# A fourth group of seven products in the feed-forward of a two-layer encoder kernel

## The chip, the cores and the metric

The kernel runs as one program on one core of one Trainium2 chip. The metric is the device time of an execution in microseconds (us), lower is better. All products are computed from float32 weights and activations, and the result must be the reference's.

## The reference

The kernel computes two layers of an encoder over 256 tokens of width 1024. Each layer has a gated linear attention, an ordinary attention, a merge of the two, a feed-forward part (FFN) and a per-layer embedding. What matters here is the FFN:

```
D_MODEL, SEQ, DEPTH = 1024, 256, 2
FFN_HIDDEN = 2816
...
gate, up = jnp.split(rms_norm(h, g_ffn_pre) @ w_ffn_in, 2, axis=-1)
h = h + rms_norm((jax.nn.silu(gate) * up) @ w_ffn_out, g_ffn_post)
```

`w_ffn_in` is 1024 x 5632 and `w_ffn_out` 2816 x 1024, for each layer. The merge before it ends in the products with `w_o_attn`, `w_o_gla` and `w_out`, each 1024 x 1024.

## The kernel before, in words

**Products.** TensorE multiplies a float32 product as three products of fp32r numbers: every operand is split into a high part and a rest, and high x high, high x low and low x high are added in one bank of PSUM (`mm3`, L99; the instruction is at L97). The program calls a product's weights `wh` and `wl`, and its accumulator `acc`.

**The stream of weights.** Nearly all weights arrive in units of 1 MB (128 x 2048 float32), in an order fixed in `plan`. The class `Stream` (L218) carries them: SyncE (SP) starts the load of a unit into a `raw` buffer (two of them, `rawp`); then ScalarE casts each half of 128 x 1024 into the high part `wh` (L113) and VectorE subtracts it for the rest `wl` (L109). These two instructions on two halves are called a split below. There are four pairs of `wh` and `wl` (`wp`), so splits run at most that far ahead of the products. A unit's products give its pair back (`done`), and then the next unit is split (`fill`) and the next load started. Tiles called `big` (128 x 2048, nine of them) and `mid` (128 x 1024, ten) hold activations and intermediate results.

**Blocks of the FFN.** The 2816 hidden columns are cut into 11 blocks of 256 (256 gate and 256 up columns). Blocks 0 and 1 are done first by token half. The others are done either as *plain* blocks, two units of 24 products of width 512 for each block, or in pairs by a *group of seven*: a pair of blocks is a 2 x 2 arrangement of weights b11, b12, b21, b22 times a 2 x 2 arrangement of activations, and instead of eight products of quarters seven are made, from sums of the quarters (Strassen's and Winograd's scheme). Each of the seven steps takes one 1 MB unit and has 12 products. The weights of the steps are, with x = b11, z = b12, y = b22, q = b21: step 1 x; step 2 x+z; step 3 x+z+y; step 4 y; step 5 z+y; step 6 q; step 7 x+z+y+q. Four *weight sums* are thus to be made for each group (`Stream.step`, L289): x+z and then +y on VectorE (one instruction each, 128 x 2048, L292); z+y by a DMA from GpSimd's queue that adds to its target (L295); and the fourth sum, +q, by two such DMAs of 512 KB each, from DRAM, issued behind step 3's split (L308). q is also loaded by itself for step 6. The sums are made in place, on raw float32 weights. x sits in a borrowed `wh` buffer and z in a borrowed `wl` (the tiles called `lent`, L244), so that three pairs are left while a group runs; y sits in a `big` tile. The next group's x may load only once `lend` is set, which is done behind step 7's split.

**The activations' side of a group** is in `seven` (L615). Step 1 adds into bank a, step 2 into bank v, steps 3 and 5 into a again, step 4 into v again, step 6 into a bank c of its own, step 7 into a once more. Between them the banks are read out: after step 1 ScalarE copies a into p1 (L629), after step 2 v into p5 (L632), after step 3 a into u (L634); after step 4 VectorE makes u = v - u, after step 5 p5 = p5 - a (both shown at L109, the helper `vsub`), after step 6 p1 = c + p1 (L625). A bank that a step adds into again must have been read before. The second step needs sums of activations (`sums`, L590), which VectorE and ScalarE make earlier. After step 6 the first token half's gate and up are complete, after step 7 the second's: SiLU on ScalarE (L1339), the product with up on VectorE (L106), and then the result is transposed (`turn_words`, L398): a copy into 16-bit words on ScalarE (L408), a transposing DMA from SP's queue (L414), a copy back on ScalarE (L427), and the split of the result into high and low for the output products. The copy back is placed behind the cast that the stream has issued last (`ws.cast`).

**Output units.** One output unit takes the 256 x 1024 rows of `w_ffn_out` that belong to one block, and has 24 products of width 512 (`out_step`, L1347). The order of blocks is `OUT`.

**The order.** The strings at the head of the program set the order of units in the FFN: `u` is a plain unit, `o` an output unit, a digit a step of a group, `p` other preparations (no unit).

```
FFN = "uu1u2u34u567" "uo12o34o5o67" "poo12o345o67"
PLAIN, PAIRS = (4, 5, 10), (2, 6, 8)
OUT = (0, 1, 2, 3, 4, 5, 10, 6, 7, 8, 9)
```

So there are three groups of seven, three plain blocks (six units), and eleven output units, of which the last three follow the string. `MERGE` is a like string, in which the products with `w_o_attn` are one more group of seven. A scheduling layer turns the program into one queue for each engine, and each queue runs strictly in its order: an instruction that waits holds all that stand behind it.

Of the kernel before, what the change touches and what calls it, by code (L numbers as in the profile page):

```python
# [37 lines left out]
PLAIN, PAIRS = (4, 5, 10), (2, 6, 8)  # L40
OUT = (0, 1, 2, 3, 4, 5, 10, 6, 7, 8, 9)

WAIT_LAST = (3, 4)
SENT, LANDED, NEXT = 3, 9, 2
# [7 lines left out]
def trunk_kernel(ctx: ExitStack, tc: tile.TileContext, a: dict, out: bass.AP):  # L52
# [25 lines left out]
    def big(dt=F32):  # L78
        return bigp.tile([P, 2048], dt, tag="big", name=nm("big"))
# [92 lines left out]
            )  # L172
        ]

    plan = []
    for l in range(DEPTH):
        w = a["w_in"][l]
        plan += [unit_rows(w, n, C_RA, C_RA + 1056, 2 if l + n == 0 else 1) for n in range(4)]
# [35 lines left out]
    class Stream:  # L214
# [8 lines left out]
        def __init__(self, depth):  # L223
# [3 lines left out]
            for item in plan:  # L227
                if callable(item):
                    x = Load(item)
                    self.loads.append(x)  # L230
                    self.jobs.append(lambda x=x: self.plain(x))
                else:
                    units, n = item
                    if n == 1:
                        b11, b12, b21, b22 = units
                        x, z = (Load(b, lambda tag=tag: self.lent(tag), tag == "wh") for b, tag in ((b11, "wh"), (b12, "wl")))
                        y, q = Load(b22, big), Load(b21)
                        pairs[id(units)] = x, y, z, q
# [12 lines left out]
        def load(self, between=lambda: None):
# [37 lines left out]
        def step(self, n, x, y, z, q):  # L289
            def add(to, other):  # L290
                c = slice(0, 2048)
                nc.vector.tensor_tensor(out=to.raw[:, c], in0=to.raw[:, c], in1=other.raw[:, c], op=ALU.add)  # L292

            def sent(to, src):
                nc.gpsimd.dma_start(to.raw[:, :2048], src, accum_op=ALU.add)  # L295

            if n == 7:
                self.load()
            self.made((x, x, x, y, z, q, x)[n - 1])
            if n == 1:  # L300
                add(x, z)
                sent(z, y.raw[:, :2048])
            elif n == 2:
                add(x, y)
            elif n == 3:
                for dst, src in q.make(x.raw):
                    for c in (slice(0, 2), slice(2, 4)):
                        nc.gpsimd.dma_start(dst[:, c], src[:, c], accum_op=ALU.add)  # L308
# [1193 lines left out]
```

## Time and profile before

| | before |
|---|---|
| time, median of 3 runs | 920.76 us (920.49 to 921.40) |
| the profiled execution's own time | 921.25 us |
| span of its profile | 919.1 us |
| TensorE's products (PE) | 904.6 us, 4561 instructions |
| VectorE (DVE) / ScalarE (ACT) busy | 737.2 / 643.9 us |
| GpSimd (POOL) busy | 112.4 us |
| chain that ended last | PE 80%, ACT 6%, DMA 5%, DVE 4% |
| DMA | 193.38 MB; hardware queue 59.3% of 16 engines' span, GpSimd's queue 10.1% |

Read it so: the span is the time from the first to the last instruction; the execution's time is 2.15 us more. Busy time of an engine is the union of its instructions, and since products overlap one another, TensorE's row lengths are longer than the distance at which products follow one another. A row of a timeline gives the start in us, the length of one in us, the engine, the line, the operation, output and inputs by the program's names (the digit in a name is the layer: `0ffnin` is layer 0's FFN), the shape, and how many instructions the row holds (x2 is two of them in succession). In square brackets stands how long the engine had been idle and what released it. A row of windows gives start and end, length, and the busy time and count of PE, PEld, DVE, ACT and POOL, then the granted clock of TensorE, the share of DMA and its GB/s. A row on DMA issues gives output and input, engine, count, size and the median time from issue to landing.

### The profile page before, as it was taken

Reading aid. Unit: us, or ns where it says so; the run is one execution under the profiler, and the core shown is the slowest. Engines: PE = TensorE matmul, PEld = TensorE weight load, DVE = VectorE, ACT = ScalarE, POOL = GpSimd, SP = SyncE. Lnnn points to the kernel's source line nnn. Section 1 sums busy time; section 2 is a strip of 40 time slices with the busy share of each in tenths; the row PEclk is TensorE's granted clock in tenths of the full one; section 3 lists DMA queues with packets and bytes.
Section 4 is the critical chain, followed back from the end, with each engine's and each line's share of the span. In section 5 each row is a group of like instructions: output and inputs, shape, how many; then the busy total and the mean of one; then the engine's idle time right before and its main releaser. Section 6 shows DMA issues by size and latency. Waiting matters only on the chain.

```text
span 919.1 us, 12313 instructions
## 1 busy us (share of the span) xinstructions
PE 904.6 (98%) x4561; PEld 768.3 (84%) x4561; DVE 737.2 (80%) x947; ACT 643.9 (70%) x1032; POOL 112.4 (12%) x174
## 2 busy tenths in 40 slices
PE   8999999999999999999999999999999999999996
PEld 6999888888888888888899988888888788878786
DVE  4798987977679796888689789688786798968874
ACT  4658777964568796776665686878656787957663
POOL 2410201140010100010023002111001010101000
PEclk9999999999999999999999999999999999999999
DMA  6555356986489998966555524399675999979541
GB/s 218 182 193 180 117 163 231 229 241 234 144 243 256 279 273 250 301 194 240 184 176 184 190 91 148 128 290 234 208 247 173 274 230 290 261 284 243 200 167 46
DMA packets 123290, 193.38 MB, mean 210 GB/s; under 512 B 33431, under 2 KB 56471, under 8 KB 122206
## 3 DMA queue, kind: packets, MB, share of 16 engines
q1 hardware_dynamic: 117726, 175.81, 59.3%
q0 software_dynamic: 5504, 16.78, 10.1%
q8 instruction: 36, 0.59, 0.3%
q14 instruction: 24, 0.20, 0.1%
HBM read 175.80 MB, written 1.05 MB: 192 GB/s over the span
## 4 chain that ended last, share of the span: by engine, by line
PE 80%; ACT 6%; DMA 5%; DVE 4%; issue 2%; POOL 2%; SPq 0%; POOLq 0%; ACTq 0%; DVEq 0%
PE acc_0ffnin L97 10%; PE acc_1ffnin L97 10%; PE acc_0ffnin L581 5%; PE acc_1gate L97 5%; PE acc_0gate L97 5%; PE acc_1ffnin L581 4%; PE acc_1gqk L97 3%; PE acc_0rq L97 2%; PE acc_0gqk L97 2%; PE acc_1ple L97 2%; PE acc_1gg L97 2%; PE acc_0gg L97 2%; PE acc_0v L97 2%; PE acc_1v L97 2%; PE acc_1merge L97 2%; PE acc_0merge L97 2%
## 5 line engine op out<-in xcount | busy, mean ns | idle before, releaser
L97 PE MATMUL acc_1ffnin<-wh_1ffnin,big_1ffnin 128*128 128x512 f32 x176 | 56.5, 392 | 0.1
L97 PE MATMUL acc_0ffnin<-wh_0ffnin,big_0ffnin 128*128 128x512 f32 x176 | 56.2, 391 | 0.0
L109 DVE TENSOR_TENSOR wl_1ffnin<-raw_1ffnin,wh_1ffnin 128x1024 fp32r<-128x1024 f32 x38 | 44.9, 1220 | 12.3 <-ACT wh_1ffnin L113 12.3
L109 DVE TENSOR_TENSOR wl_0ffnin<-raw_0ffnin,wh_0ffnin 128x1024 fp32r<-128x1024 f32 x38 | 44.9, 1221 | 10.5 <-ACT wh_0ffnin L113 10.2
L113 ACT CAST wh_1ffnin<-raw_1ffnin 128x1024 fp32r<-128x1024 f32 x38 | 38.3, 1050 | 17.7 <-DMA raw_1ffnin<-in_w_ffn_out_dram 9.1
L113 ACT CAST wh_0ffnin<-raw_0ffnin 128x1024 fp32r<-128x1024 f32 x38 | 38.4, 1050 | 16.8 <-DMA raw_0ffnin<-in_w_ffn_out_dram 7.8
L109 DVE TENSOR_TENSOR wl_1ffnin<-lent_1ffnin,wh_1ffnin 128x1024 fp32r<-128x1024 f32 x30 | 35.5, 1220 | 4.9 <-ACT wh_1ffnin L113 4.7
L109 DVE TENSOR_TENSOR wl_0ffnin<-lent_0ffnin,wh_0ffnin 128x1024 fp32r<-128x1024 f32 x30 | 35.5, 1221 | 4.8 <-ACT wh_0ffnin L113 4.7
L97 PEld LDWEIGHTS acc_1ffnin<-wh_1ffnin,big_1ffnin 128*128 128x128 f32 x176 | 33.0, 188 | 7.2 <-ACT wh_1ffnin L113 0.5
L97 PEld LDWEIGHTS acc_0ffnin<-wh_0ffnin,big_0ffnin 128*128 128x128 f32 x176 | 33.0, 188 | 6.9 <-DVE big_0ffnin L109 0.2
L113 ACT CAST wh_1ffnin<-lent_1ffnin 128x1024 fp32r<-128x1024 f32 x30 | 30.3, 1049 | 8.6 <-issue 2.9
L113 ACT CAST wh_0ffnin<-lent_0ffnin 128x1024 fp32r<-128x1024 f32 x30 | 30.3, 1050 | 8.4 <-issue 2.9
L97 PE MATMUL acc_1ffnin<-wl_1ffnin,big_1ffnin 128*128 128x512 f32 x88 | 34.4, 391 | 0.8 <-DVE wl_1ffnin L109 0.8
L97 PE MATMUL acc_0ffnin<-wl_0ffnin,big_0ffnin 128*128 128x512 f32 x88 | 34.5, 392 | 0.3 <-DVE wl_0ffnin L109 0.3
L581 PE MATMUL acc_0ffnin<-wh_0ffnin,mid_0ffnin 128*128 128x512 f32 x96 | 31.0, 390 | 0.0
L581 PE MATMUL acc_1ffnin<-wh_1ffnin,mid_1ffnin 128*128 128x512 f32 x96 | 31.0, 390 | 0.0
L97 PE MATMUL acc_0ffnin<-wh_0ffnin,big_0wout 128*128 128x512 f32 x96 | 30.4, 389 | 0.0
L97 PE MATMUL acc_1ffnin<-wh_1ffnin,big_1wout 128*128 128x512 f32 x96 | 30.3, 389 | 0.0
L97 PE MATMUL acc_0rq<-wh_start,big_start 128*128 128x384 f32 (+1 forms) x96 | 25.4, 350 | 1.5 <-ACT big_start L124 1.5
L97 PE MATMUL acc_1rq<-wh_0ple,big_0ple 128*128 128x384 f32 (+1 forms) x96 | 23.5, 325 | 0.0
L581 PE MATMUL acc_1ffnin<-wh_1ffnin,big_1wout 128*128 128x512 f32 x72 | 23.1, 389 | 0.0
L581 PE MATMUL acc_0ffnin<-wh_0ffnin,big_0wout 128*128 128x512 f32 x72 | 23.1, 389 | 0.0
(745 smaller groups left out, 3011.7 us busy)
## 6 DMA issues: line engine op xcount, KB each, us to landing
raw_0ffnin<-in_w_ffn_out_dram SPq DMA_DIRECT2D x11, 1024.0 KB, 5.1
raw_1ffnin<-in_w_ffn_out_dram SPq DMA_DIRECT2D x11, 1024.0 KB, 5.1
lent_0ffnin<-in_w_ffn_in_dram SPq DMA_DIRECT2D x6, 1024.0 KB, 7.5
lent_1ffnin<-in_w_ffn_in_dram SPq DMA_DIRECT2D x6, 1024.0 KB, 6.0
raw_0rq<-in_w_in_dram SPq DMA_DIRECT2D x4, 1024.0 KB, 5.1
raw_0v<-in_w_in_dram SPq DMA_DIRECT2D x4, 1024.0 KB, 5.1
raw_0merge<-in_w_out_dram SPq DMA_DIRECT2D x4, 1024.0 KB, 5.2
raw_0wout<-in_w_ffn_in_dram SPq DMA_DIRECT2D x8, 512.0 KB, 4.6
```

Source lines behind the costliest of these rows:

```text
L97: return nc.tensor.matmul(o, lhsT, rhs, start=start, stop=stop)
L109: nc.vector.tensor_tensor(out=out, in0=in0, in1=in1, op=ALU.subtract)
L113: cast = nc.scalar.copy(hi, src)
L581: nc.tensor.matmul(o, x, y, start=first and k + n == 0, stop=k == 3 and n == 2, skip_group_check=not first)
```

## The change

There is a fourth group of seven in each FFN, for blocks 4 and 5, which were plain. Only block 10 stays plain. Between the first steps of every group there now stand other units: a plain or an output unit behind step 1 and another behind step 2. The fourth weight sum (+q) is still made by DMAs in the first and the last group and in the merge's group (`ADDED`). In the two middle groups VectorE makes it, from q's raw buffer, behind step 5's split. x+z and x+z+y are made in two instructions of 128 x 1024, each right behind its half of the split of the step before (`made`). The groups of the FFN are `roomy`: x and z load into `big` tiles and borrow none of the four pairs, and the next x may load already behind step 6's split. The order of the output units changes with that.

```diff
-FFN = "uu1u2u34u567" "uo12o34o5o67" "poo12o345o67"
+FFN = "u1u2o34567" "1o2o34567" "p1o2o34567" "1o2o34o567"
-PLAIN, PAIRS = (4, 5, 10), (2, 6, 8)
-OUT = (0, 1, 2, 3, 4, 5, 10, 6, 7, 8, 9)
+PLAIN, PAIRS = (10,), (2, 4, 6, 8)
+ADDED = (2, 8)
+OUT = (0, 1, 10, 2, 3, 4, 5, 6, 7, 8, 9)
...
-        def lent(self, tag):
-
-            if tag == "wh":
-                self.held += 1
-                self.lend = False
+        def lent(self, tag, i):
+
+            self.lend = False
+            if i in roomy:
+                return big()
+            self.held += tag == "wh"
             return wp.tile([P, UNIT], F32R, tag=tag, name=nm("lent")).bitcast(F32)
...
-        def made(self, x):
-            for piece in self.put(x):
+        def made(self, x, other=None):
+            for j, piece in enumerate(self.put(x)):
                 self.cast = split(*piece)
+                if other:
+                    self.add(x, other, slice(j * 1024, (j + 1) * 1024))
+
+        def add(self, to, other, c=slice(0, 2048)):
+            nc.vector.tensor_tensor(out=to.raw[:, c], in0=to.raw[:, c], in1=other.raw[:, c], op=ALU.add)
...
-            self.made((x, x, x, y, z, q, x)[n - 1])
+            self.made((x, x, x, y, z, q, x)[n - 1], {1: z, 2: y}.get(n))
             if n == 1:
-                add(x, z)
                 sent(z, y.raw[:, :2048])
-            elif n == 2:
-                add(x, y)
-            elif n == 3:
+            elif n == 3 and far:
                 for dst, src in q.make(x.raw):
                     for c in (slice(0, 2), slice(2, 4)):
                         nc.gpsimd.dma_start(dst[:, c], src[:, c], accum_op=ALU.add)
-            elif n == 7:
+            elif n == 5 and not far:
+                self.add(x, q)
+            elif n == 6 and roomy_:
+                self.lend = True
+            elif n == 7 and not roomy_:
                 self.held -= 1
                 self.lend = True
```

The new arguments of `step` (`far`: the fourth sum by DMA; `roomy_`) come from two lists, filled where `plan` is made. Line numbers of the changed kernel: products of groups L589 (before L581), other products L98, casts L114, splits and subtractions L110, weight sums L298, copies of p1, p5 and u L637, L640 and L642, p1's addition L633, copy back L435.

**First pair: VectorE at the end of group 1, layer 0.** Before, `wl` 2956, 2977 and 3012 are the splits of steps 5, 6 and 7 of group 1, 3018 is that of the next plain unit; the `mid` 2815 is u, 2814 holds p1 and p5.

```order
L109 TENSOR_TENSOR wl_0ffnin_2956<-lent_0ffnin_2633,wh_0ffnin_2955 128x1024
L109 TENSOR_TENSOR mid_0ffnin_2815<-acc_0ffnin_2817,mid_0ffnin_2815 128x512
L109 TENSOR_TENSOR wl_0ffnin_2956<-lent_0ffnin_2633,wh_0ffnin_2955 128x1024
L109 TENSOR_TENSOR wl_0ffnin_2977<-raw_0ffnin_2837,wh_0ffnin_2976 128x1024 x2
L109 TENSOR_TENSOR wl_0ffnin_3012<-lent_0ffnin_2629,wh_0ffnin_3011 128x1024 x2
L109 TENSOR_TENSOR mid_0ffnin_2814<-mid_0ffnin_2814,acc_0ffnin_2816 128x512
L109 TENSOR_TENSOR wl_0ffnin_3018<-raw_0ffnin_2933,wh_0ffnin_3017 128x1024 x2
L625 TENSOR_TENSOR mid_0ffnin_2814<-acc_0ffnin_3044,mid_0ffnin_2814 128x512
```

The same place in the changed kernel: 2897 is the split of step 6, 2926 that of step 7, 2945 that of step 1 of group 2, 2972 that of an output unit; 2915 is the x and 2919 the z of group 2; 2781 is u, 2780 holds p1 and p5.

```order
L110 TENSOR_TENSOR wl_0ffnin_2897<-raw_0ffnin_2700,wh_0ffnin_2896 128x1024 x2
L110 TENSOR_TENSOR wl_0ffnin_2926<-big_0ffnin_2628,wh_0ffnin_2925 128x1024 x2
L110 TENSOR_TENSOR mid_0ffnin_2781<-acc_0ffnin_2783,mid_0ffnin_2781 128x512
L110 TENSOR_TENSOR wl_0ffnin_2945<-big_0ffnin_2915,wh_0ffnin_2944 128x1024 x2
L298 TENSOR_TENSOR big_0ffnin_2915<-big_0ffnin_2915,big_0ffnin_2919 128x1024 x2
L110 TENSOR_TENSOR big_0ffnin_2967<-mid_0ffnin_2876,big_0ffnin_2967 128x2x256
L110 TENSOR_TENSOR mid_0ffnin_2780<-mid_0ffnin_2780,acc_0ffnin_2782 128x512
L110 TENSOR_TENSOR wl_0ffnin_2972<-raw_0ffnin_2921,wh_0ffnin_2971 128x1024 x2
L633 TENSOR_TENSOR mid_0ffnin_2780<-acc_0ffnin_2979,mid_0ffnin_2780 128x512
```

The subtraction "p5 minus step 5" (`mid` 2814 before, 2780 now) stood right behind step 7's split; now the next group's first split and its first sum stand between, and a split of a transposed result.

**TensorE at the same place, changed kernel.** `wh` 2944 is step 1 of group 2, 2925 is step 7 of group 1.

```order
L589 MATMUL acc_0ffnin_2979<-wh_0ffnin_2896,big_0wout_2469 128x512
L589 MATMUL acc_0ffnin_3031<-wh_0ffnin_2944,big_0wout_2460 128x512
...
L589 MATMUL acc_0ffnin_3031<-wl_0ffnin_2945,big_0wout_2460 128x512
L589 MATMUL acc_0ffnin_2782<-wh_0ffnin_2925,big_0wout_2469 128x512
...
L589 MATMUL acc_0ffnin_2782<-wh_0ffnin_2925,big_0wout_2469 128x512
L589 MATMUL acc_0ffnin_3031<-wh_0ffnin_2944,big_0wout_2460 128x512
```

Of the 12 products of the next group's step 1, 11 stand ahead of step 7 and one behind it; before, step 7 followed step 6 directly.

**Second pair: ScalarE around the u copy in group 2, layer 0.** Before, `wh` 3259 and 3299 are output units, 3280 is step 5 and 3331 step 6 of group 2; the `mid` 3180 is u.

```order
L421 COPY mid_0ffnin_3163<-mid_0ffnin_3163 128x2x2x128 x2
L113 CAST big_0ffnin_3256<-mid_0ffnin_3163 128x2x256
L113 CAST wh_0ffnin_3259<-raw_0ffnin_3068 128x1024 x2
L634 COPY mid_0ffnin_3180<-acc_0ffnin_3181 128x512
L113 CAST wh_0ffnin_3280<-lent_0ffnin_3027 128x1024 x2
L113 CAST wh_0ffnin_3299<-raw_0ffnin_3265 128x1024 x2
L113 CAST wh_0ffnin_3331<-raw_0ffnin_3177 128x1024 x2
```

The same place in the changed kernel: 3099, 3137 and 3166 are steps 5, 6 and 7 of group 2; 3030 is u; `mid` 3039 and 3060 are the transposed results of the two token halves of group 1.

```order
L640 COPY mid_0ffnin_3029<-acc_0ffnin_3032 128x512
L114 CAST wh_0ffnin_3099<-big_0ffnin_2919 128x1024 x2
L435 COPY mid_0ffnin_3039<-mid_0ffnin_3039 128x2x512
L435 COPY mid_0ffnin_3060<-mid_0ffnin_3060 128x2x512
L114 CAST big_0ffnin_3119<-mid_0ffnin_3039 128x4x128
L114 CAST big_0ffnin_3119<-mid_0ffnin_3060 128x4x128
L114 CAST wh_0ffnin_3137<-raw_0ffnin_2977 128x1024 x2
L642 COPY mid_0ffnin_3030<-acc_0ffnin_3031 128x512
L114 CAST wh_0ffnin_3166<-big_0ffnin_2915 128x1024 x2
```

The copy of u stood ahead of the casts of steps 5 and 6. Now it stands behind both, and ahead of it stand the copies back and the casts of both transposed halves of the group before.

More of the change, by code (lines that the diff above doesn't have):

```diff
@@ L173, in unit_rows @@
         ]
-    plan = []
+    plan, added, roomy = [], [], []
     for l in range(DEPTH):
@@ L183, in trunk_kernel @@
         pair = [unit(a["w_o_attn"][l], kh, j * 512) for kh in range(2) for j in range(2)]
+        added.append(id(pair))
         for x in MERGE:
@@ L195, in trunk_kernel @@
                 pair = pairs.pop(0)
+                roomy.append(id(pair))
+                if PAIRS[-1 - len(pairs)] in ADDED:
+                    added.append(id(pair))
             plan.append(plains.pop(0) if x == "u" else outs.pop(0) if x == "o" else (pair, int(x)))
@@ L235, in __init__ @@
                         b11, b12, b21, b22 = units
-                        x, z = (Load(b, lambda tag=tag: self.lent(tag), tag == "wh") for b, tag in ((b11, "wh"), (b12, "wl")))
+                        x, z = (Load(b, lambda tag=tag, i=id(units): self.lent(tag, i), tag == "wh") for b, tag in ((b11, "wh"), (b12, "wl")))
                         y, q = Load(b22, big), Load(b21)
@@ L241, in __init__ @@
                         self.loads.append(q)
-                    self.jobs.append(lambda p=pairs[id(units)], n=n: self.step(n, *p))
-        def lent(self, tag):
-            if tag == "wh":
-                self.held += 1
-                self.lend = False
+                    self.jobs.append(lambda p=pairs[id(units)], n=n, f=id(units) in added, r=id(units) in roomy: self.step(n, f, r, *p))
+        def lent(self, tag, i):
[3 more added lines that the diff above has]
+            self.held += tag == "wh"
             return wp.tile([P, UNIT], F32R, tag=tag, name=nm("lent")).bitcast(F32)
@@ L283, in plain, with step @@
             return self.put(x)
-        def made(self, x):
-            for piece in self.put(x):
+        def made(self, x, other=None):
+            for j, piece in enumerate(self.put(x)):
                 self.cast = split(*piece)
[L289 to L292, printed above, removed]
+                if other:
+                    self.add(x, other, slice(j * 1024, (j + 1) * 1024))
+        def add(self, to, other, c=slice(0, 2048)):
+            nc.vector.tensor_tensor(out=to.raw[:, c], in0=to.raw[:, c], in1=other.raw[:, c], op=ALU.add)
+        def step(self, n, far, roomy_, x, y, z, q):
             def sent(to, src):
```

## The prediction

> **What bounds the kernel now.** I read the page's busy times, then the windows over the first layer's FFN, then the timelines of TensorE, VectorE, ScalarE and GpSimd in that stretch, and last the landing times of its DMAs.
>
> ```profile
> PE 904.6 (98%) x4561; PEld 768.3 (84%) x4561; DVE 737.2 (80%) x947; ACT 643.9 (70%) x1032; POOL 112.4 (12%) x174
> 280.00:326.40 46.40, 46.40 (x206) 38.45 (x205) 40.59 (x44) 37.50 (x52) 3.42 (x3) 1.00 0.97 253
> 326.40:375.00 48.60, 48.33 (x213) 39.73 (x212) 39.78 (x39) 36.14 (x44) 3.29 (x3) 1.00 0.92 285
> ```
>
> TensorE has next to no gaps here (46.40 of 46.40 us, then 48.33 of 48.60), VectorE is busy for 82 to 87%, and the granted clock is 1.00. What a product costs is read from where units of products begin, since the 0.39 us of one overlaps the next:
>
> ```profile
> 291.06 0.39 PE L581 MATMUL acc_0ffnin<-wh_0ffnin,big_0wout 128*128 128x512 f32 x1
> ...
> 293.78 0.39 PE L97 MATMUL acc_0ffnin<-wh_0ffnin,big_0wout 128*128 128x512 f32 x1
> ...
> 299.22 0.39 PE L581 MATMUL acc_0ffnin<-wh_0ffnin,mid_0ffnin 128*128 128x512 f32 x1
> ```
>
> A step of a group (12 products) takes 293.78 - 291.06 = 2.72 us, a plain unit (24) 5.44 us, so one product 0.2267 us. An output unit has 24 too.
>
> **What is removed.** Two plain blocks are 4 units x 24 = 96 products, a group of seven is 7 x 12 = 84. That is 12 fewer per layer, 24 in all: 24 x 0.2267 = 5.44 us off TensorE, all of it on the path as long as TensorE does not wait. This is the only gain.
>
> **What VectorE gets instead.** Every unit, whatever its number of products, needs a split of two 128x1024 halves on VectorE. Its prices, by starts of successive instructions:
>
> ```profile
> 287.21 2.28 DVE L292 TENSOR_TENSOR lent_0ffnin<-lent_0ffnin,lent_0ffnin 128x2048 f32<-128x2048 f32 x1
> 289.41 0.69 DVE L109 TENSOR_TENSOR mid_0ffnin<-mid_0wout,mid_0ffnin 128x512 fp32r<-128x512 f32 x1
> 290.01 0.42 DVE L109 TENSOR_TENSOR big_0ffnin<-mid_0ffnin,big_0ffnin 128x256 fp32r<-128x256 f32 x1
> 290.34 2.35 DVE L109 TENSOR_TENSOR wl_0ffnin<-raw_0ffnin,wh_0ffnin 128x1024 fp32r<-128x1024 f32 x2
> 292.61 0.42 DVE L109 TENSOR_TENSOR big_0ffnin<-mid_0ffnin,big_0ffnin 128x256 fp32r<-128x256 f32 x1
> ```
>
> So a sum of weights costs 2.20 us, a 512-wide operation 0.60, a 256-wide one 0.33, a split 2.27. A sum in two halves isn't in the trace; I take a split's 2.27, the same two widths (bounds 2.20, as one piece, and 2 x 1.22 = 2.44, with no overlap).
>
> Seven more splits and four fewer are 3 x 2.27 = 6.8 us per layer; the new group's two sums are 4.5, and the two middle groups' sums of q 4.4: 15.7 us more VectorE work, in 2.72 us less time. By groups, counted from the order of the changed kernel:
>
> Group 1 (u1u2o34567): TensorE 3 x 5.44 + 7 x 2.72 = 35.4; VectorE 10 splits 22.7, two sums 4.5, seven 512-wide 4.2, eight 256-wide 2.7 = 34.1. Groups 2 and 3 (1o2o34567): TensorE 2 x 5.44 + 19.0 = 29.9; VectorE 9 splits 20.4, three sums 6.7, eight 512-wide 4.8 = 31.9. Group 4: TensorE 35.4; VectorE 22.7 + 4.5 + 4.2 = 31.4.
>
> So the middle groups ask 2.0 us more of VectorE than TensorE lasts. Against this stands lead: groups of the FFN no longer borrow one of the four hi/lo buffers, so splits may run a unit further ahead. What the lead is worth is decided at three places, where a queue in strict order makes TensorE wait.
>
> **Wait 1: end of group 1.** Step 7 adds into the bank that VectorE's "p5 minus step 5" reads, so it waits for that. Before, this subtraction stands right behind step 7's own split. Now a split, a sum and another operation stand between (first pair of order blocks), and step 7's split itself waits for q, still added by DMA in this group.
>
> ```profile
> 302.28 2.47 POOL L308 DMA_DIRECT2D lent_0ffnin<-in_w_ffn_in_dram  x2 [11.27 <-DVE wl_0ffnin L109]
> 307.38 0.39 PE L581 MATMUL acc_0ffnin<-wh_0ffnin,mid_0ffnin 128*128 128x512 f32 x1
> L308 POOL DMA_DIRECT2D lent_0ffnin<-in_w_ffn_in_dram x6: 1194/1229/1347, 302.3 to 392.4; - x6
> lent_0ffnin<-in_w_ffn_in_dram POOLq DMA_DIRECT2D x2, 512.0 KB, 10.3
> DMA to landing us min/median/max: 6.1/9.1/13.6
> 299.42 2.00 ACT L113 CAST wh_0ffnin<-lent_0ffnin 128x1024 fp32r<-128x1024 f32 x2 [0.30 <-PE acc_0ffnin L97]
> ```
>
> The DMA begins 5.1 us ahead of TensorE's step 3 (302.28 to 307.38); with the longer lead I take 5.5. From step 3 on, TensorE has steps 3 to 6 and 11 of the 12 products of the next group's step 1: 5.5 + 10.9 + 2.5 = 18.9 us until it needs the subtraction. (Before, a plain unit of 5.44 us lay in between and the 11 products did not: 21.4.) The chain: second half issued after 1.2, landed 10.3 later (this group's row) 11.5, cast 1.05, split's second half 1.2, one 512-wide 0.6, next split 2.27, sum 2.27, two 512-wide 1.2 = 20.2. TensorE waits 1.3 us. With the landings of the row's ends (6.1, 13.6) it is 0 and 4.6.
>
> [...]
>
> **Waits 2 and 3: step 5 of groups 2 and 3.** Step 5 adds into a bank that ScalarE must first copy (u). Before, the copy stood ahead of the casts of steps 5 and 6; now it stands behind step 6's cast, which stands behind two results that a DMA transposes (second pair of order blocks).
>
> ```profile
> 329.20 1.04 ACT L408 COPY t_0ffnin<-t_0ffnin 128x1024 uint16<-128x1024 uint16 x1
> 339.41 1.37 ACT L427 COPY mid_0ffnin<-mid_0ffnin 128x1024 uint16<-128x1024 uint16 x1
> 340.63 0.58 ACT L629 COPY mid_0ffnin<-acc_0ffnin 128x512 f32<-128x512 f32 x1
> 341.10 0.63 ACT L113 CAST big_0ffnin<-mid_0ffnin 128x512 fp32r<-128x512 f32 x1
> 341.62 2.01 ACT L113 CAST wh_0ffnin<-lent_0ffnin 128x1024 fp32r<-128x1024 f32 x2
> 343.52 1.36 ACT L427 COPY mid_0ffnin<-mid_0ffnin 128x1024 uint16<-128x1024 uint16 x1
> mid_0ffnin<-t_0ffnin SPq DMA_TRANSPOSE x11, 5.1
> mid_1ffnin<-t_1ffnin SPq DMA_TRANSPOSE x11, 6.8
> 394.99 0.60 PE L1367 MATMUL aux_0emb<-ident,mid_0ffnin 128*128 128x128 f32 x4
> ```
>
> Group 2, from the moment step 7 of group 1 begins. VectorE: three splits 6.8, one sum 2.27, three 512-wide 1.8 = 10.9 until the second half's gate product. ScalarE: the cast it is in 0.5, the copy to words 1.04 = 12.4. Landing 5.1 in layer 0, 6.8 in layer 1: 17.5 or 19.2. Then the copy back 1.22, two casts 1.04, step 6's cast 1.90, u 0.58: 22.3 or 23.9. TensorE arrives after 2.72 + 0.23 + 5.44 + 2.72 + 5.44 + 2.72 + 2.72 = 22.0. It waits 0.3 and 1.9: 1.1 on average. Group 3 has its first sum inside the stretch (2.27) and half a cast more (0.2); TensorE has 0.6 of other work first, three more products 0.7 and the four 128x128 transposes 0.6: 24.8 or 26.4 against 23.9, waits of 0.9 and 2.5, 1.7 on average. A transpose landing 2 us sooner takes both away; bounds 0 and, with 4 us more, 4.8 and 5.2.
>
> **What costs nothing.** Group 4 has 4.0 us of VectorE to spare, so the lead returns there, and the tail of three output units is as before. The bytes loaded stay the same; accumulating DMAs stay at six per FFN (z four times, q twice, where both were three). These queues have room in the longer groups; where they had none, a 1 MB load would come some 5 us late, which the second buffer of raw weights hides. The attention pair gets its two sums in halves (0.07 each): hidden by TensorE there, 0.3 us in all if not.
>
> **The sum.** The profiled execution took 921.25 us: a span of 919.1 and 2.15 around it; it lies 0.49 above the median, and I apply the difference to the median. Waits 1.3 + 1.1 + 1.7 = 4.1 per layer, 8.2 in all, against 5.44: 2.8 us more. 920.76 + 2.8 = 923.5.
>
> **The rivals.** *The lead holds.* None of the three waits appears: 920.76 - 5.44 = 915.3, and up to 917.5 with 1.1 us of waiting per layer. For it: four of the six waits (two layers) are below 1.4 us, within what my bounds leave open, and casts of before sat waiting for a buffer (299.42, released by PE), which one more buffer ends. Against: VectorE is over its time in two groups. Chance 0.30.
>
> *One of the two kinds of DMA is quick.* Transposes land in 5.1 us in both layers: 1.3 + 0.3 + 0.9 = 2.5 per layer, 5.0 in all, 920.3; or the sum of q lands in 6.1: 2.8 per layer, 920.9. No change. Chance 0.22, of which 0.06 for the second, since 6.1 is the shortest of its row. [...]
>
> *VectorE becomes the bound of the middle groups.* With no lead left at the end of group 1, TensorE goes as VectorE goes: 4.0 us over, and each of 18 splits may wait for its cast as these do:
>
> ```profile
> 346.82 2.36 DVE L109 TENSOR_TENSOR wl_0ffnin<-big_0ffnin,wh_0ffnin 128x1024 fp32r<-128x1024 f32 x2 [0.25 <-ACT wh_0ffnin L113]
> 350.68 2.36 DVE L109 TENSOR_TENSOR wl_0ffnin<-raw_0ffnin,wh_0ffnin 128x1024 fp32r<-128x1024 f32 x2 [0.26 <-ACT wh_0ffnin L113]
> ```
>
> 18 x 0.25 = 4.5; with wait 1 it is 9.8 per layer, 19.6 - 5.44 = 14.2 more: 934.9. It decides once wait 1 is over 2 us. Against it: the lead, and that not every split waits. Chance 0.13. [...]
>
> **How the numbers follow.** My forecast has 0.35, the lead 0.30, the quick DMA 0.22, VectorE 0.13. About 0.2% (1.8 us) is what a measurement of this kernel can tell from no change: faster 0.30, same 0.22, slower 0.35 + 0.13 = 0.48. The range runs from the full gain, 915.0, to 931.0, where two of the waits are near their upper bounds; what lies above it is most of the last rival.
>
> **What would show it.** TensorE's products down by 24, VectorE's busy time up by some 31 us. Idle time of PE ahead of L589 products, released by DVE mid_0ffnin at the end of group 1 (about 1.3 us) and by ACT L642 at step 5 of groups 2 and 3, larger in layer 1. I am wrong if PE's idle time in the two FFNs stays under 3.6 us, if it sits at other places, or if VectorE has no idle time left in groups 2 and 3.

## The result and the profile after

The changed kernel takes 933.78 us (median of 4 runs, 932.09 to 937.40) against 920.85 us (4 runs, 920.49 to 921.40): a ratio of 1.0152, 95% interval 1.0132 to 1.0171. It is slower, as forecast, but by 12.9 us and not by 2.8, and it lies above the range. The profiled execution has a span of 932.6 us, 13.5 more than before.

First the busy times of the page, then TensorE's waits (engine, line, what it waited for, us in all, times, longest):

```profile
PE 904.9 (97%) x4537; PEld 765.1 (82%) x4537; DVE 768.8 (82%) x989; ACT 657.0 (70%) x1042; POOL 109.8 (12%) x172
```

```profile
PE acc_1ffnin L98 <- ACT big_1ffnin L114: 5.2, 1, 5.2
PE acc_0ffnin L98 <- ACT big_0ffnin L114: 4.4, 1, 4.4
PE acc_1ffnin L589 <- ACT mid_1ffnin L642: 2.3, 2, 1.8
...
PE acc_1ffnin L589 <- DVE mid_1ffnin L110: 1.3, 1, 1.3
PE acc_0ffnin L589 <- DVE mid_0ffnin L110: 1.2, 1, 1.2
PE acc_0ffnin L589 <- ACT mid_0ffnin L642: 0.9, 1, 0.9
```

There are 24 products fewer (4561 to 4537) and 31.6 us more of VectorE, as worked out. The last four rows are the three forecast waits: together 5.7 us where 8.2 was forecast. The two on top, 9.6 us, were not forecast at all. They stand at one place, in each layer once: the output unit of block 6, the third output unit of group 4. Where TensorE stops there and where that unit ends (the next row of each pair is the first product of step 5):

```profile
402.76 0.80 PE L98 MATMUL acc_0ffnin<-wh_0ffnin,big_0ffnin 128*128 128x512 f32 x1 [4.42 <-ACT big_0ffnin L114]
411.02 0.39 PE L589 MATMUL acc_0ffnin<-wh_0ffnin,mid_0ffnin 128*128 128x512 f32 x1
...
862.11 0.79 PE L98 MATMUL acc_1ffnin<-wh_1ffnin,big_1ffnin 128*128 128x512 f32 x1 [5.18 <-ACT big_1ffnin L114]
869.42 0.39 PE L589 MATMUL acc_1ffnin<-wh_1ffnin,mid_1ffnin 128*128 128x512 f32 x1
```

The unit itself takes 8.26 and 7.31 us, where 24 products took 5.44. The windows of one microsecond in layer 0 show why (the column ahead of the last two is the granted clock):

```profile
398.00:399.00 1.00, 0.34 (x2) 0.00 (x0) 0.00 (x0) 0.00 (x0) 0.00 (x0) 1.00 1.37 54
...
400.00:401.00 1.00, 0.00 (x0) 0.00 (x0) 0.00 (x0) 0.09 (x1) 0.00 (x0) 1.00 1.15 227
401.00:402.00 1.00, 0.00 (x0) 0.00 (x0) 0.00 (x0) 1.00 (x1) 0.00 (x0) 0.82 1.07 234
402.00:403.00 1.00, 0.23 (x1) 0.24 (x2) 0.26 (x1) 1.00 (x3) 0.00 (x0) 0.50 1.05 307
...
407.00:408.00 1.00, 1.00 (x3) 0.76 (x3) 1.00 (x2) 1.00 (x2) 0.00 (x0) 0.50 0.27 86
408.00:409.00 1.00, 1.00 (x5) 0.76 (x4) 1.00 (x2) 1.00 (x2) 0.00 (x0) 0.77 0.03 8
```

TensorE is idle from 398.34, the clock falls to 0.50 at about 401.6 and is back at about 408.5, long after the products go on. What released TensorE is found by the chain of waits, by ScalarE's timeline and by the queues of SP and GpSimd in layer 0, in this order:

```profile
389.94 10.95 DMA mid_0ffnin<-t_0ffnin
```

```profile
393.13 1.37 ACT L435 COPY mid_0ffnin<-mid_0ffnin 128x1024 uint16<-128x1024 uint16 x1
400.91 1.33 ACT L435 COPY mid_0ffnin<-mid_0ffnin 128x1024 uint16<-128x1024 uint16 x1 [6.41 <-DMA mid_0ffnin<-t_0ffnin]
402.11 1.12 ACT L114 CAST big_0ffnin<-mid_0ffnin 128x512 fp32r<-128x512 f32 x2
```

```profile
389.94 1.23 SPq L422 DMA_TRANSPOSE mid_0ffnin<-t_0ffnin  x1
```

```profile
390.11 2.45 POOL L312 DMA_DIRECT2D big_0ffnin<-in_w_ffn_in_dram  x2 [11.83 <-ACT t_0ffnin L416]
```

The second half of group 3's result is sent to be transposed at 389.94. At 390.11 GpSimd starts the two DMAs that add q for group 4. The transpose takes 10.95 us (11.71 in layer 1). ScalarE stands idle for 6.41 us at the copy back, and behind it in its queue stand the casts of both halves of the result (402.11), which the output unit needs.

The whole, counted from each FFN's first product to the first transpose behind it on TensorE: 174.9 and 175.9 us before, 181.7 and 184.3 after, 15.2 more. The terms: products -5.44; waits 6.52 in layer 0 (4.42, 1.24 and 0.86) and 8.74 in layer 1 (5.18, 2.27 and 1.29), less the 0.27 and 0.76 that before had there; the block 6 unit at the lower clock, 2.82 and 1.87. That is 13.5; the other 1.7 us are short delays that the list of waits does not show. The rest of the program was 1.7 us shorter in this execution (2.8 shorter up to the first FFN, whose first product starts at 253.39 and not at 256.21), so 13.5 in all.

### The profile page after: what moved, and what is told of

Its sections match the earlier page's. It is cut to its first block, busy times and chain, and to the rows that moved or that the text cites. A ratio compares the mean times of both kernels' runs of the same rounds, so it can differ in the third digit from the quotient of the medians.

```text
span 932.6 us, 12323 instructions
## 1 busy us (share of the span) xinstructions
PE 904.9 (97%) x4537; PEld 765.1 (82%) x4537; DVE 768.8 (82%) x989; ACT 657.0 (70%) x1042; POOL 109.8 (12%) x172
## 4 chain that ended last, share of the span: by engine, by line
PE 63%; DVE 11%; DMA 11%; ACT 8%; issue 4%; POOL 2%; SPq 0%; ACTq 0%; POOLq 0%; DVEq 0%
PE acc_1ffnin L98 6%; PE acc_0gate L98 5%; PE acc_0ffnin L98 4%; PE acc_1gate L98 4%; PE acc_1ffnin L589 3%; PE acc_0ffnin L589 3%; DVE wl_0ffnin L110 3%; DMA mid_1ffnin<-t_1ffnin 3%; PE acc_1gqk L98 2%; PE acc_0gqk L98 2%; PE acc_1ple L98 2%; PE acc_1gg L98 2%; PE acc_0gg L98 2%; PE acc_1v L98 2%; PE acc_0v L98 2%
## 5 line engine op out<-in xcount | busy, mean ns | idle before, releaser
L98 PE MATMUL acc_1ffnin<-wh_1ffnin,big_1ffnin 128*128 128x512 f32 x176 | 58.0, 400 | 5.3 <-ACT big_1ffnin L114 5.2
L98 PE MATMUL acc_0ffnin<-wh_0ffnin,big_0ffnin 128*128 128x512 f32 x176 | 58.5, 404 | 4.4 <-ACT big_0ffnin L114 4.4
L114 ACT CAST wh_1ffnin<-big_1ffnin 128x1024 fp32r<-128x1024 f32 x48 | 49.1, 1052 | 13.4 <-DVE big_1ffnin L298 10.8
L114 ACT CAST wh_0ffnin<-big_0ffnin 128x1024 fp32r<-128x1024 f32 x48 | 49.0, 1051 | 13.2 <-DVE big_0ffnin L298 10.5
L110 DVE TENSOR_TENSOR wl_0ffnin<-big_0ffnin,wh_0ffnin 128x1024 fp32r<-128x1024 f32 x48 | 56.2, 1219 | 1.6 <-ACT wh_0ffnin L114 1.6
L110 DVE TENSOR_TENSOR wl_1ffnin<-big_1ffnin,wh_1ffnin 128x1024 fp32r<-128x1024 f32 x48 | 56.2, 1219 | 1.2 <-ACT wh_1ffnin L114 1.2
L98 PEld LDWEIGHTS acc_1ffnin<-wh_1ffnin,big_1ffnin 128*128 128x128 f32 x176 | 33.9, 193 | 13.1 <-ACT big_1ffnin L114 6.1
L98 PEld LDWEIGHTS acc_0ffnin<-wh_0ffnin,big_0ffnin 128*128 128x128 f32 x176 | 34.2, 195 | 12.2 <-ACT big_0ffnin L114 4.8
L589 PE MATMUL acc_1ffnin<-wh_1ffnin,mid_1ffnin 128*128 128x512 f32 x128 | 41.6, 392 | 2.3 <-ACT mid_1ffnin L642 2.3
L589 PE MATMUL acc_0ffnin<-wh_0ffnin,mid_0ffnin 128*128 128x512 f32 x128 | 41.5, 391 | 0.9 <-ACT mid_0ffnin L642 0.9
L110 DVE TENSOR_TENSOR wl_1ffnin<-raw_1ffnin,wh_1ffnin 128x1024 fp32r<-128x1024 f32 x34 | 40.2, 1219 | 1.9 <-ACT wh_1ffnin L114 1.8
L110 DVE TENSOR_TENSOR wl_0ffnin<-raw_0ffnin,wh_0ffnin 128x1024 fp32r<-128x1024 f32 x34 | 40.2, 1220 | 1.5 <-ACT wh_0ffnin L114 1.3
L114 ACT CAST wh_1ffnin<-raw_1ffnin 128x1024 fp32r<-128x1024 f32 x34 | 34.2, 1048 | 6.3 <-DVE mid_1ffnin L110 2.4
L114 ACT CAST wh_0ffnin<-raw_0ffnin 128x1024 fp32r<-128x1024 f32 x34 | 34.2, 1050 | 5.1 <-PE acc_0ffnin L98 1.8
L98 PE MATMUL acc_0ffnin<-wl_0ffnin,big_0ffnin 128*128 128x512 f32 x88 | 35.2, 400 | 0.0
L98 PE MATMUL acc_1ffnin<-wl_1ffnin,big_1ffnin 128*128 128x512 f32 x88 | 35.0, 398 | 0.0
L589 PE MATMUL acc_1ffnin<-wh_1ffnin,big_1wout 128*128 128x512 f32 x96 | 30.8, 392 | 1.4 <-DVE mid_1ffnin L110 1.3
L589 PE MATMUL acc_0ffnin<-wh_0ffnin,big_0wout 128*128 128x512 f32 x96 | 30.8, 392 | 1.3 <-DVE mid_0ffnin L110 1.2
L589 PEld LDWEIGHTS acc_1ffnin<-wh_1ffnin,mid_1ffnin 128*128 128x128 f32 x128 | 24.0, 188 | 8.3 <-ACT mid_1ffnin L642 2.9
L589 PEld LDWEIGHTS acc_0ffnin<-wh_0ffnin,mid_0ffnin 128*128 128x128 f32 x128 | 24.0, 188 | 6.7 <-ACT mid_0ffnin L642 1.6
L589 PE MATMUL acc_0ffnin<-wl_0ffnin,mid_0ffnin 128*128 128x512 f32 x64 | 24.9, 389 | 0.0
L589 PE MATMUL acc_1ffnin<-wl_1ffnin,mid_1ffnin 128*128 128x512 f32 x64 | 24.9, 389 | 0.0
```

What stands on the lines that cost most here:

```text
L98: return nc.tensor.matmul(o, lhsT, rhs, start=start, stop=stop)
L110: nc.vector.tensor_tensor(out=out, in0=in0, in1=in1, op=ALU.subtract)
L114: cast = nc.scalar.copy(hi, src)
L589: nc.tensor.matmul(o, x, y, start=first and k + n == 0, stop=k == 3 and n == 2, skip_group_check=not first)
```

## The experiments

The first theory: the DMAs that add q in the last group collide with the transpose, and the wait and the half clock follow. The rival: VectorE is the bound, and the results come late for that reason. It had this for it (windows of after; VectorE is the fifth column from the left, with its count in brackets):

```profile
310.00:390.00 80.00, 77.76 (x341) 63.23 (x340) 79.99 (x79) 63.85 (x75) 2.58 (x3) 1.00 0.82 237
```

**The sum left out, or given to VectorE, in the last group.** The first leaves part of the computation out.

```diff
+NONE = (8,)
...
-f=id(units) in added
+f=None if id(units) in none else id(units) in added
...
-            elif n == 5 and not far:
+            elif n == 5 and far is False:
```

> The fourth weight sum (+q) of the last group is left out, so step 7 of that group multiplies with x+z+y alone; nothing takes its place. Collision theory: with the two adding DMAs gone, the transposed second half lands in 5 to 6 us and not in 10.95, the wait at block 6's output unit is under 0.5 us, the clock stays at 1.00: 918 to 921. Rival (the results leave VectorE and ScalarE late, the DMA is not what counts): the wait stays over 3 us in each layer and the time above 928.

```diff
-ADDED = (2, 8)
+ADDED = (2,)
```

> The fourth sum of the last group is made on VectorE, as in the two middle groups; that of the first group stays with the DMA. Collision theory: as without the sum, less what 2.2 us more of VectorE in group 4 cost (4 us were to spare there): 918 to 922. Rival (VectorE is the bound): 4.4 us more on the bound, over 934.

Without the sum 920.63 us (918.68 to 931.02; ratio 1.0017, 0.9994 to 1.0040), with it on VectorE 923.80 us (918.27 to 929.30; 1.0032, 1.0009 to 1.0056). In both the waits at block 6's unit are gone; the second time lies 1.8 us above the range that was expected. The same transpose in layer 1 with the sum on VectorE, from the chain:

```profile
842.74 5.33 DMA mid_1ffnin<-t_1ffnin
```

5.33 us against 11.71, and with 2.2 us more of VectorE in each layer the kernel is 10 us faster, where the rival has it slower. So the DMA is what counts in group 4. The runs of both kernels scatter over more than 10 us, though, and the profiled execution of the kernel without the sum, the longest of its runs (931.02), shows where (TensorE in layer 0, then ScalarE):

```profile
312.00 0.79 PE L592 MATMUL acc_0ffnin<-wh_0ffnin,mid_0ffnin 128*128 128x512 f32 x1 [6.37 <-ACT mid_0ffnin L645]
```

```profile
306.65 0.76 ACT L438 COPY mid_0ffnin<-mid_0ffnin 128x512 uint16<-128x512 uint16 x1 [6.24 <-DMA mid_0ffnin<-t_0ffnin]
```

It is a collision of the same kind in group 1, where q is still added by DMA: there a copy back of a transposed result holds ScalarE, and u's copy, which step 5 needs, stands behind it. The transpose that lands so late was issued at 291.39 and took 15.25 us. In the profile of the changed kernel the one at this place has the same DMAs beside it and took 7.34 us, so their presence alone does not say how long it takes. The profiled execution with the sum on VectorE, one of the shortest of its runs (920.62), has no such wait in group 1; that it is this which parts the runs is likely from these two profiles, not shown for each run.

**The sum by DMA in all groups.** If the collision is the cause, giving it to the middle groups must cost much, although VectorE gets lighter.

```diff
-ADDED = (2, 8)
+ADDED = (2, 4, 6, 8)
```

> The fourth sum is made by DMA in all four groups, none on VectorE (4.4 us less of VectorE per layer). Collision theory: in groups 2 and 3 the adding DMAs now meet the transposes of the group before, too, whose copies back hold ScalarE's copy of u, so that TensorE waits some 4 to 5 us at step 5 in both groups of both layers, partly with the half clock behind it: 940 to 965. Rival (VectorE is the bound): 933.8 less up to 8.8, 925 to 930.

952.07 us (943.59 to 955.67; 1.0330, 1.0292 to 1.0368), with TensorE waiting at step 5 of groups 2 and 3 in both layers (first and last row; the middle one is block 6's unit in layer 1):

```profile
PE acc_1ffnin L589 <- ACT mid_1ffnin L642: 6.5, 2, 4.8
PE acc_1ffnin L98 <- ACT big_1ffnin L114: 6.2, 1, 6.2
PE acc_0ffnin L589 <- ACT mid_0ffnin L642: 6.0, 2, 4.1
```

The places and the time are those of the collision theory, and VectorE as the bound would have made it faster. The sizes were forecast less well: 4 to 5 us everywhere, where it was 4.1 and 4.8 in group 2 and 1.8 and 1.7 in group 3.

**Any DMA, or the adding?** The sum is left out of the last group as above, and q is brought to the same place without being added; step 7 there multiplies with q alone.

```diff
+            elif n == 3 and far is None:
+                for dst, src in q.make(x.raw):
+                    for c in (slice(0, 2), slice(2, 4)):
+                        nc.gpsimd.dma_start(dst[:, c], src[:, c])
```

> The changed kernel, but in the last group of each feed-forward GpSimd's two DMAs of 512 KB bring q to the same place, at the same point, without adding it: step 7 of that group multiplies with q alone. If it is the adding that crowds out the transpose, the transposed half lands in 5 to 7 us and the time is that without the sum, 918 to 922; if any 1 MB that lands at that moment does it, the transpose still takes over 9 us and the time stays above 929.

936.20 us (934.79 to 936.74; 1.0174, 1.0161 to 1.0187). The transposes of the two layers, from the chain:

```profile
390.92 11.62 DMA mid_0ffnin<-t_0ffnin
...
851.73 10.88 DMA mid_1ffnin<-t_1ffnin
```

So it is not the adding: here 1 MB that GpSimd's queue moves at that moment is enough. Loads on SP's queue, on which the transposes stand too, need not do it: in layer 1 of the changed kernel the transpose issued at 816.48 has one load of 1 MB ahead of it (814.95) and three behind it (from 817.76), and lands in 4.71 us. Whether 1 MB on a third queue would was not tried.

**Moving the one who waits.** Block 6's output unit goes behind step 7; and then the copies back of all transposed results of the FFN go further back on ScalarE too.

```diff
-FFN = "u1u2o34567" "1o2o34567" "p1o2o34567" "1o2o34o567"
+FFN = "u1u2o34567" "1o2o34567" "p1o2o34567" "1o2o34567o"
```

> The third output unit of the last group (block 6) is moved from behind step 4 to behind step 7. Collision theory: TensorE's waits of 4.42 and 5.18 us at this unit come from the second half of group 3's result, whose transposing DMA was issued at 389.94 us beside the DMAs that add q (390.11) and landed at 400.89; 8.2 us of steps 5 to 7 now cover it, and the 6 us of products at a granted clock of 0.50 behind each wait (about 5 us in all) go with it: 933.8 - 9.6 - 5 = 919.2, between 917.5 and 921.5. Rival (VectorE, busy 10.00 of 10 us from 310 to 390, is the bound): the lost time comes back as waits for VectorE at other units of group 4, and the time stays above 929.

```diff
-            yield LANDED
+            yield LANDED + (6 if far else 0)
```

> As the kernel with the late output unit, and the copies back of transposed results stand further behind on ScalarE: in group 4 behind the casts of steps 6 and 7 and the copy of u instead of ahead of them. The DMAs still collide. If what costs is that ScalarE waits at the head of its queue for the transposed half with step 6's cast behind it, the waits of 5.84 and 6.60 us at step 6 go; step 7 is then held by the late sum itself, some 3 us with part of the half clock: 926 to 932, against 939 with the late output unit alone. Rival (TensorE waits for the output unit's data or for VectorE): 937 or more.

Both expectations failed; the times lie where the rivals had them, though VectorE is not what TensorE waits for. The late unit gives 939.22 us (936.51 to 949.88; 1.0224, 1.0185 to 1.0263), with TensorE's wait now at step 6:

```profile
405.85 0.79 PE L589 MATMUL acc_0ffnin<-wh_0ffnin,big_0wout 128*128 128x512 f32 x1 [5.84 <-ACT wh_0ffnin L114]
```

I had taken the wait for one of the output unit for its data. It is one of ScalarE at the head of its queue: step 6's cast stands behind the copy back as well, and waits with it whoever is next on TensorE. With the copies further back it is 950.27 us (944.09 to 951.98; 1.0327, 1.0312 to 1.0342): now ScalarE waits for q's own sum at step 7's cast, and the copies back stand behind that, so that TensorE waits 5.2 and 4.8 us at products of an output unit:

```profile
408.84 1.04 ACT L114 CAST wh_0ffnin<-big_0ffnin 128x1024 fp32r<-128x1024 f32 x1 [4.12 <-DMA big_0ffnin<-in_w_ffn_in_dram]
409.79 1.33 ACT L435 COPY mid_0ffnin<-mid_0ffnin 128x1024 uint16<-128x1024 uint16 x1
```

Both DMAs of the collision land late, and each order puts one of the two landings ahead of something that TensorE needs.

**The half clock.** 44 transposes of the identity fill the wait; nothing reads them.

```diff
+            if n == 6 and hf == 0:
+                ps = aux()
+                for i in range(44):
+                    nc.tensor.transpose(ps[:, :P], ident, ident)
```

> The changed kernel with 44 transposes of 128x128 of the identity ahead of block 6's output unit in each layer, so that TensorE works through the wait; nothing reads their result. If the clock of 0.50 comes from TensorE having been idle, it stays at 1.00 in both layers, and the products behind the wait take 5.4 and not 8.4 us: 933.8 less 4 to 5, 928 to 931. Rival (the clock falls for another reason): no gain, 933 to 937.

934.49 us (929.54 to 942.16; 1.0165, 1.0128 to 1.0202). The profile is of the longest of its four runs (942.16). The clock is 1.00 through the wait and through the unit behind it in both layers, and in layer 1 the unit takes 876.07 - 870.51 = 5.56 us and not 7.31:

```profile
865.79 4.97 PE L1362 MATMUL aux_1ffnin<-ident 128*128 128x128 f32 x44
870.51 0.48 PE L98 MATMUL acc_1ffnin<-wh_1ffnin,big_1ffnin 128*128 128x512 f32 x1
876.07 0.39 PE L589 MATMUL acc_1ffnin<-wh_1ffnin,mid_1ffnin 128*128 128x512 f32 x1
...
882.02 0.47 PE L589 MATMUL acc_1ffnin<-wh_1ffnin,big_1wout 128*128 128x512 f32 x1 [0.35 <-DVE mid_1ffnin L110]
...
887.41 0.66 PE L448 MATMUL aux_1ffnin<-ident,t_1ffnin 128*128 128x128 f32 x4 [1.04 <-DVE t_1ffnin L107]
```

So in the changed kernel the clock falls to 0.50 because TensorE was idle for 4.42 and 5.18 us. But the time did not get better: ScalarE and VectorE were held up as well, and TensorE, faster, waits for them at 882.02 and 887.41. From the unit's start to the 887.41 row it is 16.90 us, in the changed kernel 17.44 (862.11 to 879.55): of the 1.75 us gained, 0.54 is left. Even that is not a gain, since the last of the 44 transposes held the unit up. Counted from the start of the copy back, when the late transpose has landed (868.17 here, 860.25 in the changed kernel), the two are level, 19.24 and 19.30 us; in layer 0 it is 20.09 (405.48 to 425.57) against 19.63 (400.91 to 420.54). So the 2.82 and 1.87 us above are time that passed at the lower clock, not what removing that alone would save.

**What is left without any collision.** All fourth sums of the FFNs go to VectorE; then two read-outs are put earlier in their queues (p5 minus step 5 on VectorE, the copy of u on ScalarE); then GpSimd's own adder makes the sums.

```diff
-ADDED = (2, 8)
+ADDED = ()
```

> The fourth sum is made on VectorE in all four groups of each feed-forward; only the merge's group keeps the DMAs. Collision theory: with the sum of group 1 off GpSimd's queue too, no transposed result has an adding DMA beside it in any group: the runs lie closer together than those with the last group's sum on VectorE alone (918.3 to 929.3), at 916 to 920. Rival (VectorE is the bound): 4.4 us more of VectorE per layer, over 926.

```diff
+        def early(f, *args):
+            with tc.high_priority(AHEAD):
+                f(*args)
...
-        times(a, form(1), False, lambda: nc.scalar.copy(u, a))
+        times(a, form(1), False, lambda: early(nc.scalar.copy, u, a))
...
-        times(a, form(3), False, lambda: vsub(p5, p5, a))
+        times(a, form(3), False, lambda: early(vsub, p5, p5, a))
```

> As the kernel with all fourth sums on VectorE, and the two read-outs that TensorE waits for are put earlier in their engines' queues: VectorE's p5 minus step 5 ahead of the next group's first split and sum, ScalarE's copy of u ahead of step 6's cast. Theory: the waits of 0.96, 0.79, 0.92, 1.14, 1.01 and 0.26 us of that kernel (5.1 us) are what eats the 5.44 us of saved products, and they go: 921.85 less 3 to 5, 916.5 to 919, under the kernel before. Rival (VectorE, busy without a gap from 310 to 390 us, is the bound in these groups, and the waits only show it): they come back at the splits, 921 to 923.

```diff
-                self.add(x, q)
+                for c in (slice(0, 1024), slice(1024, 2048)):
+                    nc.gpsimd.tensor_tensor(out=x.raw[:, c], in0=x.raw[:, c], in1=q.raw[:, c], op=ALU.add)
```

> As the kernel with the two read-outs put earlier, but GpSimd's own adder makes the fourth sum of all four groups, in two halves, so that neither VectorE (2.2 us less in each group) nor a DMA has it. VectorE is busy 39.75 and 39.78 of 40 us from 320 to 400 us in that kernel. If VectorE is the bound of the groups there, the waits fall from 6.6 to under 2 us and the time to 916 to 918.5, under the kernel before. Rival: GpSimd's addition is slow or slows VectorE beside it, so that step 7 waits for it: over 925.

All on VectorE: 921.85 us (920.47 to 926.30; 1.0031, 1.0015 to 1.0048). No fourth sum of an FFN is left to collide, and the runs lie closer, but the time is between what the theory (916 to 920) and the rival (over 926) gave, and not under the kernel before. The two FFNs take 175.2 and 175.9 us, 351.1 together against 350.8 before, and TensorE waits in them at the three forecast places (the first and last two rows), and little elsewhere:

```profile
PE acc_0ffnin L589 <- ACT mid_0ffnin L642: 1.7, 2, 0.9
...
PE acc_1ffnin L589 <- ACT mid_1ffnin L642: 1.3, 2, 1.0
PE acc_1ffnin L589 <- DVE mid_1ffnin L110: 1.1, 1, 1.1
PE acc_0ffnin L589 <- DVE mid_0ffnin L110: 1.0, 1, 1.0
```

That is 5.1 us, and 0.4 for a split of layer 1: in this execution the saved 5.44 us are given back here. With the read-outs earlier it is 922.30 us (917.90 to 923.88; 1.0014, 1.0001 to 1.0027). The waits for u are gone, and there are new ones for the splits behind:

```profile
PE acc_0ffnin L589 <- DVE mid_0ffnin L110: 1.7, 1, 1.7
...
PE acc_1ffnin L98 <- DVE wl_1ffnin L110: 1.5, 3, 0.6
PE acc_0ffnin L98 <- DVE wl_0ffnin L110: 1.5, 3, 0.6
```

```profile
320.00:400.00 80.00, 78.31 (x341) 63.20 (x342) 79.53 (x78) 63.79 (x74) 2.71 (x3) 1.00 0.89 253
```

VectorE is busy 79.53 of 80 us, TensorE 78.31: the rival's answer. With GpSimd's adder it is 936.37 us (936.01 to 938.71; 1.0191, 1.0177 to 1.0205). One half of a sum takes it 2.35 to 7.79 us, the longest beside splits of VectorE that run at their usual 1.21 us. In other places VectorE is the one held up (GpSimd's row, then VectorE's):

```profile
327.64 10.58 POOL L315 TENSOR_TENSOR big_0ffnin<-big_0ffnin,raw_0ffnin 128x1024 f32<-128x1024 f32 x2 [10.72 <-DVE wl_0ffnin L110]
```

```profile
334.75 4.02 DVE L110 TENSOR_TENSOR big_0ffnin<-mid_0ffnin,big_0ffnin 128x512 fp32r<-128x512 f32 x2 [1.58 <-ACT big_0ffnin L114]
```

The same two instructions in the kernel with the read-outs put earlier:

```profile
338.81 1.29 DVE L110 TENSOR_TENSOR big_0ffnin<-mid_0ffnin,big_0ffnin 128x512 fp32r<-128x512 f32 x2
```

4.02 us against 1.29, with GpSimd's two rows (327.64 to 338.22) beside them for 3.47 of the 4.02. Why it is now GpSimd that is held up and now VectorE, no run shows.

**The rest of the change without the fourth group.** Strings, plain blocks, pairs and output order as before, the fourth sum by DMA in all three groups.

```diff
+FFN = "uu1u2u34u567" "uo12o34o5o67" "poo12o345o67"
+PLAIN, PAIRS = (4, 5, 10), (2, 6, 8)
+ADDED = (2, 6, 8)
+OUT = (0, 1, 2, 3, 4, 5, 10, 6, 7, 8, 9)
```

> Everything of the change but the fourth group: order strings, plain blocks and output order of the kernel before, x and z in their own tiles, sums in halves, the fourth sum by DMA in all three groups. Collision theory: the adding DMAs and the transposes lie as far apart as in the kernel before: 918 to 922. Rival (the tiles, the halved sums or the earlier loads are what costs): over 926.

928.76 us (five runs, 923.95 to 930.36; a sixth took 942.46; 1.0082, 1.0060 to 1.0105): missed, and inside the rival's range. The profiled execution (924.72) has no wait at any of the places spoken of; its longest are 1.7 us in layer 1 and 4.0 us behind layer 0's FFN:

```profile
PE aux_0ffnout L448 <- DVE h L546: 4.0, 1, 4.0
```

There VectorE's queue has splits of the next weights ahead of the residual's sum. The changed kernel has no such wait; what the longer runs of this kernel wait for was not seen. So this run says only that the tiles, the halved sums and the earlier loads are not free by themselves, not where their price lies in the changed kernel. Nor do the adding DMAs and the transposes lie apart in it, as was expected. In the middle group they start together (SP's queue, then GpSimd's):

```profile
341.57 2.26 SPq L422 DMA_TRANSPOSE mid_0ffnin<-t_0ffnin  x1
341.59 2.41 POOL L312 DMA_DIRECT2D big_0ffnin<-in_w_ffn_in_dram  x2 [8.05 <-DVE wl_0ffnin L110]
```

This transpose lands after 8.68 us, the one at this place in layer 1 after 7.90, and no wait of TensorE follows. In this execution a collision thus costs nothing by itself; in the changed kernel what needs the landing stands close behind it.

## Why the prediction was wrong

**Right:** the sign; the 24 products; 31.6 us more of VectorE (some 31); VectorE as the busier of the two in the middle groups (79.99 of 80 us against 77.76); and the three places at which TensorE would wait. Their sizes, forecast and measured:

| | forecast, layer 0 / 1 | measured, layer 0 / 1 |
|---|---|---|
| wait 1, end of group 1 | 1.3 / 1.3 | 1.24 / 1.29 |
| wait 2, step 5 of group 2 | 0.3 / 1.9 | 0 / 1.82 |
| wait 3, step 5 of group 3 | 0.9 / 2.5 | 0.86 / 0.45 |

Two of the three signs that it named for being wrong came as well: idle time of TensorE at other places, and no idle time left of VectorE in groups 2 and 3.

**Right size, wrong reason:** wait 1 was worked out through the landing of q's sum. Without that DMA in group 1 the wait at this place is still 0.96 and 1.14 us. What is late is VectorE, which has no gap there; the order of its queue alone is not it either, since with the subtraction put ahead 1.70 and 0.87 remain. (The chain of wait 1 also adds up to 20.1 and not 20.2 us, and 4 us on top of waits 2 and 3 would be 5.1 and 5.7 on average, not 4.8 and 5.2; neither changes the result.)

**The step that failed** is "What costs nothing". It counted the adding DMAs, found six as before and room in their queues, and priced them only by a load that would come late. It did not ask what else is in flight when they start. Before, plain units lay between the groups, so the results of one group were transposed well ahead of the next one's fourth sum (in layer 0 the last group of before sent its sum at 391, when no transpose had been started since 380). Now group 4 follows group 3 without them, and the split of step 3, behind which the sum is issued, falls into the same microsecond as the copy into words ahead of the transpose. It also said that group 4 has VectorE time to spare and "the lead returns there"; the place that costs most is in group 4. In its place the runs showed a transpose of 10.95 and 11.71 us, 9.6 us of waits behind it and 4.7 us of half clock behind those. Removing the DMA there takes 13.2 us off the median (933.78 to 920.63), more than the whole loss. A sign of it could be read in the profile of before: the transpose issued at 379.92, beside a z sum on GpSimd's queue (from 381.67), took 8.9 us, where the median of its row was 5.1.

The half clock behind a wait was in no term. It was not to be seen in the profile of before, in whose middle TensorE never waits for more than 0.76 us.

**The rivals:** "VectorE becomes the bound" gave 934.9, nearly the measured time, by a mechanism that was not the one that cost it. That the two numbers are close is luck. VectorE was the bound in the middle groups, and its price is seen in the kernel without these collisions, whose VectorE has still more to do: about the 5.44 us saved and 1.6 us more (921.85 against 920.26 for the kernel before, taken alongside). "One of the two kinds of DMA is quick" looked at the same transposes and asked only whether they would be quicker.

**Open:** which of the executions have the collision in group 1, and why; what the tiles and halved sums cost by themselves; the 1.7 us in short delays.

## What to carry to other kernels

When a change moves work closer together, list for each transfer not only who waits for it but what else is in flight when it starts: here the adding DMAs stayed at six, and one transpose took 11.71 us beside two of them and 5.33 without. ScalarE, in its strict order, waited 6.41 us for such a landing and held everything behind it, so the wait showed up at whatever came next: moving the consumer moved the wait (5.84 us at step 6, then 5.2 and 4.8 at products of an output unit), and only leaving out the transfer or giving its work to VectorE ended it (920.63 and 923.80 us). And products saved on one engine were worth nothing where another was already busy for the same time: 5.44 us less of TensorE, VectorE busy for 79.53 of 80 us, and 922.30 us against 919.86 for the kernel before, taken alongside.

## What the runs showed of the hardware

- The transpose by DMA of the second half of group 3's result (128 x 1024 words) lands in 4.7 to 6.4 us in the five kernels of four groups that have no DMA of q in the last one, and in 8.1 to 13.7 us in the six that have it (2 x 512 KB on GpSimd's queue, added or not; 10.6 to 11.8 in the four that leave groups 2 and 3 and the copies back as in the changed kernel).
- TensorE's clock falls to 0.50 behind a wait and stays there for about 6.8 us in the changed kernel (401.6 to 408.5; 859.0 to 865.9). In the profiles of this study all waits from 3.36 us on were followed by it and none up to 1.82; of thirteen between 1.83 and 2.37 eight were. One of these, with the last group's sum on VectorE:

```profile
313.00:314.00 1.00, 0.06 (x1) 0.00 (x0) 1.00 (x2) 1.00 (x3) 0.00 (x0) 1.00 0.00 0
314.00:315.00 1.00, 0.00 (x0) 0.00 (x0) 1.00 (x3) 0.92 (x1) 0.52 (x1) 1.00 0.00 0
315.00:316.00 1.00, 0.90 (x3) 0.70 (x4) 1.00 (x2) 0.00 (x0) 0.35 (x1) 0.68 0.42 82
316.00:317.00 1.00, 1.00 (x4) 0.81 (x3) 1.00 (x2) 0.00 (x0) 0.00 (x0) 0.50 0.90 188
317.00:318.00 1.00, 1.00 (x3) 0.77 (x3) 1.00 (x3) 0.05 (x1) 0.00 (x0) 0.50 1.28 254
318.00:319.00 1.00, 1.00 (x4) 0.80 (x3) 1.00 (x2) 0.58 (x1) 0.00 (x0) 0.61 0.70 131
```

That is a wait of 2.04 us, and behind it 3.4 us at 0.50 (the shortfall of the clock column, 0.32 + 0.50 + 0.50 + 0.39 = 1.71, over 0.50). The lengths at 0.50 behind a wait were 3.4 and 6.8 us and in two kernels 10.2: once, twice and three times 3.413. In each trace the changes of the clock lie whole multiples of 3.413 us apart (in the changed kernel it is down at 401.64, up at 408.47 and down at 859.03: 2 and 132 times 3.413). With each of the thirteen traces divided on this grid, from 20 us on, the clock fell at the end of every stretch of 3.413 us at full clock that had TensorE idle for 1.83 us or more, and of none that had it idle for 1.79 us or less. So a wait of about 2 us was followed by the half clock where all of it or nearly all lay within one stretch, and not where two shared it. The two waits of 2.37 us, both with GpSimd's adder, show it: of the first, 1.97 us lay in one stretch, and the clock fell at 345.39; of the second, ending at 831.81, 0.64 us lay in one and 1.73 in the next, and the clock stayed at 1.00.
